# Linear attention on one core: all seven levels of a head prepared first, one run of score products, odd tiles of the coarsest level in the other column half

## The chip, the cores and the metric

The kernel runs on 1 core of one Trainium2 chip. The metric is device time in microseconds (us), the median of several runs. A core has a matrix engine (TensorE, in the profile PE, with its weight loads as PEld), a vector engine (VectorE, DVE), a scalar engine (ScalarE, ACT), a general engine (GpSimd, POOL) and a queue engine (SyncE, SP). They run side by side, each through its own queue in order, and wait for one another by semaphores. TensorE writes to PSUM, eight banks of 128 partitions by 512 float32 numbers; everything else lies in SBUF.

## The reference, cut to what matters

A decoder trunk of two layers on 512 tokens of width 1024, in float32. Each layer has a half-step SwiGLU feed-forward block, a mixer, and a second feed-forward block. The first layer's mixer is gated linear attention with 4 heads (128 key columns, 256 value columns), the second's is stick-breaking attention. The change is in the first mixer:

```python
bc = jnp.cumsum(to_chunks(log_a, GLA_HK), axis=3)      # per key column, a running log decay
...
o_inter = jnp.einsum('bhtk,bhkv->bhtv', q_t * jnp.exp(b_t), state)
diff = b_t[:, :, :, None, :] - b_t[:, :, None, :, :]
decay = jnp.exp(jnp.where(causal[:, :, None], diff, -jnp.inf))
scores = jnp.einsum('bhtk,bhtsk,bhsk->bhts', q_t, decay, k_t)
o_intra = jnp.einsum('bhts,bhsv->bhtv', scores, v_t)
```

The score of query t and key s is a sum over 128 key columns of q times k times exp(b_t - b_s), for s up to t. The decay differs by column, so the scores are not a plain product of two matrices unless the exponent is split at a reference point between s and t.

## The kernel before

**Tiles.** The kernel works on 4 tiles of 128 tokens (NT = 4), transposed: 128 key columns on the partitions, 512 tokens along the free axis. Within a tile of 128 the scores are a triangle of 128 by 128, and the kernel cuts it into *levels* (LEVELS = 64, 32, 16, 8, 4, 2, 1). At level B the tile falls into pieces of 2B tokens; the queries of a piece's second half meet the keys of its first half, and the last token of the first half is the reference. What is left is the diagonal, t = s.

**prepare(B)** (line 1164) makes one tile e of 128 by 512 for a level: two subtractions of b from its reference (lines 1172, 1173), an exponential on ScalarE (line 656, called from 1174), and two multiplications, the first halves by k and the second halves by q (lines 1175, 1176). Tiles named e come from a pool of 6 buffers with the tag "e", which the output's temporaries (kd, osq, sh, sl, vv) share.

**level(ps, e, B)** (line 1183) takes the score products. A bank of PSUM holds two levels, 256 columns each. For each of 4 tiles and each half of 64 keys (c = 0 or 64) one product of 128 by 64 weights with 64 columns is written to partitions c to c + 63, so that the two calls of a pair use the two column halves of the matrix engine. At level 64 only the first 64 tokens are keys, and there is one call a tile, with c = 0. Products are in float32, and a call shows as two rows in the profile, since the kernel's other products are of rounded high and low parts (float32r) that show as one.

**pick(ps, li)** (line 1189) copies, under a mask of zeros and ones, what a level gives into the score tile S (128 by 4 by 128) on VectorE. The diagonal is a product with the identity (line 1215), also on VectorE, and level 64 fills a block of 64 by 64 in each tile by a copy on ScalarE (line 1221).

**A head's turns.** levels(h) is a generator with 8 yields (n = 0 to 7), and the loop in run() (lines 1373 to 1399) puts work between them. At each n it runs one stretch of levels(h), then, from n = 1 on, one stretch of the previous head's output(), then one feed step: 24 products of the projections that are still to come (v, the gates). The feed keeps TensorE busy while VectorE prepares. Before the change the stretches are: n = 0 to 2 prepare levels 64, 32, 16; n = 3 takes the diagonal and these three levels in two z banks, prepares level 8, and empties the banks; n = 4 to 6 prepare levels 4, 2, 1; n = 7 takes the last four levels in two z banks and empties them.

**output(h)** (line 1235) runs one head later: kd and its exponentials, transposes of kd into the o bank (ps_kd, n = 3), the state products in the o bank and a z bank (ps_s, n = 5) with the running states on VectorE (lines 1279, 1281), the output products with S (ps_o, t banks, n = 7), then the norm (ps_on, o bank; vv, y, on). The last head's output has the output projection (ps_b) as its feed.

**PSUM.** Of the eight banks the tag a has 2, z 3, t 2 and o 1.

**Order.** The queues are laid out ahead of the run by a planner that simulates the engines: it goes by the order of the program, and where an instruction isn't ready by its own times it puts a later one first. Pieces of weights are cut into high and low parts by ScalarE (wh, line 152) and VectorE (wl, line 153) as the feed needs them.

Of the kernel before, what the change touches and what calls it, by code (L numbers as in the profile page):

```python
# [10 lines left out]
F32 = mybir.dt.float32  # L11
F32R = mybir.dt.float32r
# [6 lines left out]
P = 128  # L19
T = 512  # L20
# [3 lines left out]
NT = T // P  # L24
# [22 lines left out]
def decoder(ctx: ExitStack, tc: tile.TileContext, a: dict, out: bass.AP):  # L47
    nc = tc.nc
# [976 lines left out]
    class GLA:  # L1025
# [61 lines left out]
        def gate_weights(self):  # L1087

            gr = self.ep.tile([P, KD, 16], F32, tag="gr", bufs=1, name="gr")
            with nc.allow_non_contiguous_dma("gate columns"):  # L1090
                nc.gpsimd.dma_start(gr, cols(self.w_in, 3072, 16))
            self.gs = gs = self.ep.tile([P, KD, P], F32R, tag="gs", bufs=1, name="gs")
            nc.gpsimd.memset(gs.bitcast(F32), 0.0)
            nc.scalar.copy(gs[:, :, 0:16], gr)
            nc.vector.tensor_tensor(
                out=gs[:, :, 32:48], in0=gr, in1=gs[:, :, 0:16].bitcast(F32), op=ALU.subtract
            )

# [12 lines left out]
            one = self.ep.tile([P, 64], F32R, tag="one", bufs=1, name="one")[:, 0:1]  # L1111
            nc.scalar.copy(one, gT[:, 50:51])
            self.ones = one.to_broadcast([P, P])
            self.tri = self.ep.tile([P, P], F32, tag="tri", bufs=1, name="tri")
            nc.gpsimd.dma_start(self.tri, a["c_tri"])
            lf = self.ep.tile([P, len(LEVELS) * P // 2], F32, tag="e", name="lf")
            nc.gpsimd.dma_start(lf, a["c_lvl"])
            self.lvl = self.ep.tile([P, len(LEVELS) * P // 2], U8, tag="lvl", bufs=1, name="lvl")
            nc.vector.tensor_copy(self.lvl, lf)
            self.ga = self.gp.tile([P, T], F32R, tag="g", name="ga")  # L1120
            nc.gpsimd.memset(self.ga.bitcast(F32), 1.0)
# [7 lines left out]
        def gate_logits(self):  # L1129
            ga, t = self.ga, self.ep.tile([P, T], F32, tag="e", name="gl")  # L1130
            nc.vector.tensor_tensor(
# [25 lines left out]
        def levels(self, h):  # L1157
# [6 lines left out]
            def prepare(B):  # L1164
# [3 lines left out]

                e = self.ep.tile([P, T], F32, tag="e", name="e")
                (b0, b1), (e0, e1) = halves(b), halves(e)  # L1170
# [12 lines left out]
            def level(ps, e, B):  # L1183
                r = ps.rearrange("p (n m c) -> p n m c", n=NT, c=B)
                for i in range(NT):
                    for c in (0,) if B == H else (0, H):
                        mm(r[c : c + H, i], e[:, i * P + c : i * P + c + H], seconds(e, B)[:, i], True, True)

# [12 lines left out]
            es = []  # L1201
            for B in LEVELS[0:3]:
                es.append(prepare(B))
                yield
            halves = [t[:, c : c + T // 2] for t in (psum("ps_S", "z"), psum("ps_S", "z")) for c in (0, T // 2)]
            for i in range(NT):
# [3 lines left out]
            for ps, e, B in zip(halves[1:], es, LEVELS):  # L1210
                level(ps, e, B)
            es = [prepare(LEVELS[3])]
            for c in (0, H):
# [6 lines left out]
                )  # L1220
            nc.scalar.copy(S[0:H, :, H:P], halves[1][0:H].rearrange("p (n c) -> p n c", n=NT))
            pick(halves[2], 1)
            pick(halves[3], 2)
            yield
            for B in LEVELS[4:]:
                es.append(prepare(B))
                yield
            halves = [t[:, c : c + T // 2] for t in (psum("ps_S", "z"), psum("ps_S", "z")) for c in (0, T // 2)]
            for ps, e, B in zip(halves, es, LEVELS[3:]):
                level(ps, e, B)  # L1230
            for li, ps in enumerate(halves):
                pick(ps, li + 3)
            yield

        def output(self, h):
# [3 lines left out]
            bl = b.rearrange("p (n s) -> p n s", n=NT)[:, :, P - 1 : P]  # L1239
            kd = ep.tile([P, T], F32, tag="e", name="kd")  # L1240
            nc.vector.tensor_tensor(
# [46 lines left out]
            for vb in range(2):  # L1288
# [7 lines left out]
                po.append(ps)  # L1296
            sq, t = (ep.tile([P, T], F32, tag="e", name="osq") for _ in range(2))
# [4 lines left out]
            sh = ep.tile([P, T], F32R, tag="e", name="sh")  # L1302
            sl = ep.tile([P, T], F32R, tag="e", name="sl")
            nc.scalar.copy(sh, sq)
# [4 lines left out]
            mm(ps, self.ones, turns(sl), False, True)  # L1309
            vv = ep.tile([P, T], F32, tag="e", name="vv")  # L1310
            nc.vector.tensor_scalar(
# [687 lines left out]
```

## Time and profile before

| | us |
|---|---|
| median of 3 runs | 1762.55 |
| lowest and highest of these | 1762.22 and 1762.95 |
| the profiled execution | 1762.8 |
| its span, by the profile | 1760.9 |

All rows quoted below are from the profiled execution, and their times count from the start of its span. A row of a timeline has the start, the length, the engine, the line of the code, the operation, what is written from what, the shapes, and how many such instructions follow one another without a break; behind it stands, in brackets, how long the engine was idle just ahead and what ended that. Rows of products overlap, since a product starts before the one ahead has left the array; how fast they come is read from their starts. A row of stretches has the limits, the length, the busy time of each engine with its instructions, the granted clock of TensorE, and the DMA engines' share and rate. Rows of a group have the shortest, median and longest duration in ns.

### The profile page before, as it was taken

The numbers are of one execution on the slowest core, as the hardware profiler recorded it, in microseconds if no ns is written. First come the engines' busy times: TensorE is split into PE (matmuls) and PEld (weight loads), VectorE is DVE, ScalarE is ACT, GpSimd is POOL, SyncE is SP. The second block draws the span as 40 slices with busy tenths as digits, with TensorE's granted clock in tenths as the row PEclk, the third lists the DMA queues.
The fourth block names the chain that finished last, engine by engine and source line by source line (L and its number), as shares of the span: only waits on it lengthen the run. The fifth ranks groups of instructions, "written<-read, shape, count | busy, mean of one in ns | idle before, by whom it ended". The sixth has DMA issues, their size and how long they took to land.

```text
span 1760.9 us, 31387 instructions
## 1 busy us (share of the span) xinstructions
PE 1749.1 (99%) x12714; PEld 1631.3 (93%) x12714; DVE 1509.2 (86%) x2490; ACT 1063.8 (60%) x1899; POOL 55.6 (3%) x77
## 2 busy tenths in 40 slices
PE   9999999999999999999999999999999999999998
PEld 8999999889888999999989999999888889999997
DVE  8999797786888999889798988977898679998886
ACT  7556556554665565555655555655888755565555
POOL 0000000200000000000000000010000000000000
PEclk9999999999999999999999999999999999999999
DMA  5533435422123443444434344352212234434351
GB/s 169 155 113 116 134 107 148 116 65 70 60 79 113 122 118 121 120 121 126 128 98 134 103 126 129 106 133 84 84 49 73 72 96 132 126 102 124 117 146 52
DMA packets 186389, 193.14 MB, mean 110 GB/s; under 512 B 4931, under 2 KB 171125, under 8 KB 186245
## 3 DMA queue, kind: packets, MB, share of 16 engines
q1 hardware_dynamic: 177760, 175.91, 32.0%
q0 software_dynamic: 8240, 14.95, 4.7%
q8 instruction: 99, 1.62, 0.4%
q14 instruction: 46, 0.37, 0.1%
q10 hardware_dynamic: 244, 0.29, 0.0%
HBM read 175.17 MB, written 2.10 MB: 101 GB/s over the span
## 4 chain that ended last, share of the span: by engine, by line
PE 89%; DVE 7%; ACT 3%; DMA 1%; issue 1%; DVEq 0%; SPq 0%
PE ps_w L779 21%; PE ps_d L80 15%; PE ps_f L80 14%; PE ps_q L779 10%; PE ps_z L779 5%; PE ps_w L412 5%; PE ps_b L80 4%; PE ps_t L80 4%; PE ps_q L412 2%; PE ps_z L412 1%; DVE wl L153 1%; PE ps_z L1486 1%; PE ps_oT L1572 1%; PE ps_bt L80 1%; PE ps_T L1557 1%; DMA raw<-in_ffn_w_gate_dram 1%
## 5 line engine op out<-in xcount | busy, mean ns | idle before, releaser
L153 DVE TENSOR_TENSOR wl<-raw,wh 128x1024 fp32r<-128x1024 f32 x241 | 256.4, 1065 | 37.0 <-ACT wh L152 36.2
L152 ACT CAST wh<-raw 128x1024 fp32r<-128x1024 f32 x241 | 222.2, 923 | 70.0 <-PE ps_f L80 23.6
L153 DVE TENSOR_TENSOR wl<-s,wh 128x1024 fp32r<-128x1024 f32 x160 | 195.8, 1224 | 66.2 <-ACT wh L152 65.3
L779 PE MATMUL ps_w<-th,wh 128*128 128x256 f32 x864 | 239.1, 277 | 0.2 <-ACT ps_z L807 0.2
L779 PE MATMUL ps_w<-tl,wh 128*128 128x256 f32 x864 | 237.8, 275 | 0.0
L779 PE MATMUL ps_w<-th,wl 128*128 128x256 f32 x864 | 237.8, 275 | 0.0
L152 ACT CAST wh<-s 128x1024 fp32r<-128x1024 f32 x160 | 168.8, 1055 | 6.0 <-DVE s L765 6.0
L779 PEld LDWEIGHTS ps_w<-th,wh 128*128 128x128 f32 x864 | 165.9, 192 | 1.1 <-ACT ps_z L807 0.4
L80 PE MATMUL ps_f<-xh,wh 128*128 128x512 f32 x432 | 166.5, 386 | 0.0
L779 PEld LDWEIGHTS ps_w<-tl,wh 128*128 128x128 f32 x864 | 166.0, 192 | 0.0
L779 PEld LDWEIGHTS ps_w<-th,wl 128*128 128x128 f32 x864 | 166.0, 192 | 0.0
L80 PE MATMUL ps_f<-xh,wl 128*128 128x512 f32 x432 | 164.3, 380 | 0.5 <-DVE wl L153 0.5
L80 PE MATMUL ps_f<-xl,wh 128*128 128x512 f32 x432 | 164.0, 380 | 0.0
L80 PE MATMUL ps_d<-hh,wh 128*128 128x512 f32 x416 | 157.9, 380 | 0.0
L80 PE MATMUL ps_d<-hh,wl 128*128 128x512 f32 x416 | 157.8, 379 | 0.0
L80 PE MATMUL ps_d<-hl,wh 128*128 128x512 f32 x416 | 157.8, 379 | 0.0
L153 DVE TENSOR_TENSOR wl<-rawd,wh 128x1024 fp32r<-128x1024 f32 (+1 forms) x100 | 96.6, 966 | 9.7 <-ACT wh L152 9.7
L807 ACT COPY ps_z<-ps_w 128x256 f32<-128x256 f32 x72 | 26.0, 362 | 118.3 <-PE ps_w L779 118.1
L363 POOL DMA_DIRECT2D x<-d x53 | 46.0, 911 | 1552.1 <-ACT d L362 1093.5
L80 PEld LDWEIGHTS ps_f<-xl,wh 128*128 128x128 f32 x432 | 81.8, 189 | 11.4
L80 PEld LDWEIGHTS ps_f<-xh,wl 128*128 128x128 f32 x432 | 81.8, 189 | 11.3 <-DVE wl L153 0.9
L80 PEld LDWEIGHTS ps_f<-xh,wh 128*128 128x128 f32 x432 | 81.8, 189 | 10.7
(357 smaller groups left out, 5437.9 us busy)
## 6 DMA issues: line engine op xcount, KB each, us to landing
raw<-in_ffn_w_gate_dram SPq DMA_DIRECT2D x43, 1024.0 KB, 5.5
raw<-in_ffn_w_up_dram SPq DMA_DIRECT2D x43, 1024.0 KB, 5.4
rawd<-in_ffn_w_down_dram SPq DMA_DIRECT2D x84, 512.0 KB, 4.0
x<-d POOLq DMA_DIRECT2D x53, 256.0 KB, 4.6
raw<-in_gla_w_in_dram SPq DMA_DIRECT2D x12, 1024.0 KB, 5.3
raw<-in_sb_w_in_dram SPq DMA_DIRECT2D x16, 512.0 KB, 3.7
raw<-in_gla_w_out_dram SPq DMA_DIRECT2D x4, 1024.0 KB, 5.4
raw<-in_sb_w_in_dram SPq DMA_DIRECT2D x4, 1024.0 KB, 5.1
```

The lines of the kernel that those rows point to most:

```text
L80: st["pe"] = nc.tensor.matmul(ps, l, r, start=first, stop=last).ins
L152: nc.scalar.copy(h[:, k], part)
L153: nc.vector.tensor_tensor(out=l[:, k], in0=part, in1=h[:, k].bitcast(F32), op=ALU.subtract)
L363: nc.gpsimd.dma_start(xs[k], d, accum_op=ALU.add)
L412: st["pe"] = nc.tensor.matmul(ps, l_, r_, start=first and c + n == 0, stop=c == 1 and n == 2, skip_group_check=True).ins
L779: st["pe"] = nc.tensor.matmul(o, l_, r_, start=first and j + n == 0, stop=j == 3 and n == 2, skip_group_check=True).ins
L807: v["copied"] = nc.scalar.copy(z, w).ins
L1486: nc.tensor.matmul(o_, l_, r_, start=first, stop=last, skip_group_check=True)
L1557: nc.tensor.transpose(ps[:, c0 : c0 + P], ys[yb][:, yc + j * P : yc + (j + 1) * P], ident)
L1572: nc.tensor.matmul(po[e * 64 : e * 64 + 64, j * P : T], self.v[j][:, c : c + 64], self.wt[p, e][bk][:, c0 : c0 + n], start=j == 0, stop=j ...
```

## The change

All seven levels are prepared at n = 0 to 6, one at a time. At n = 7 the diagonal and all seven levels are multiplied in one run, into eight halves of four banks: three z banks and the o bank. Then the diagonal is written, ScalarE copies level 64, and the picks follow with levels 2 and 1 first (li = 5 and 6, the o bank), then levels 32 to 4.

Level 64 now writes the scores of tiles 1 and 3 to partitions 64 to 127, tiles 0 and 2 as before, so that its calls go to the two column halves in turn. The copy is in two pieces: even tiles from the lower partitions, odd tiles from the upper ones.

The pool with the tag "e" has 8 buffers in place of 6, which takes 4 KB more of each partition. Every use of the tag names the number.

```diff
-                e = self.ep.tile([P, T], F32, tag="e", name="e")
+                e = self.ep.tile([P, T], F32, tag="e", bufs=8, name="e")
...
             def level(ps, e, B):
                 r = ps.rearrange("p (n m c) -> p n m c", n=NT, c=B)
                 for i in range(NT):
-                    for c in (0,) if B == H else (0, H):
-                        mm(r[c : c + H, i], e[:, i * P + c : i * P + c + H], seconds(e, B)[:, i], True, True)
+                    for c in (0, H):
+                        if B < H:
+                            mm(r[c : c + H, i], e[:, i * P + c : i * P + c + H], seconds(e, B)[:, i], True, True)
+                        elif c == i % 2 * H:
+                            mm(r[c : c + H, i], e[:, i * P : i * P + H], seconds(e, B)[:, i], True, True)
...
             es = []
-            for B in LEVELS[0:3]:
+            for B in LEVELS:
                 es.append(prepare(B))
                 yield
-            halves = [t[:, c : c + T // 2] for t in (psum("ps_S", "z"), psum("ps_S", "z")) for c in (0, T // 2)]
+            halves = [t[:, c : c + T // 2] for t in (psum("ps_S", tag) for tag in "zzzo") for c in (0, T // 2)]
             for i in range(NT):
                 for c in (0, H):
                     s = slice(i * P + c, i * P + c + H)
                     mm(halves[0][c : c + H, i * H : i * H + H], k[:, s], q[:, s], True, True)
             for ps, e, B in zip(halves[1:], es, LEVELS):
                 level(ps, e, B)
-            es = [prepare(LEVELS[3])]
             for c in (0, H):
...
-            nc.scalar.copy(S[0:H, :, H:P], halves[1][0:H].rearrange("p (n c) -> p n c", n=NT))
-            pick(halves[2], 1)
-            pick(halves[3], 2)
-            yield
-            for B in LEVELS[4:]:
-                es.append(prepare(B))
-                yield
-            halves = [t[:, c : c + T // 2] for t in (psum("ps_S", "z"), psum("ps_S", "z")) for c in (0, T // 2)]
-            for ps, e, B in zip(halves, es, LEVELS[3:]):
-                level(ps, e, B)
-            for li, ps in enumerate(halves):
-                pick(ps, li + 3)
+            for c in (0, H):
+                to, of = (
+                    t.rearrange("p (n two) c -> p two n c", two=2)[:, c // H]
+                    for t in (S[0:H, :, H:P], halves[1][c : c + H].rearrange("p (n c) -> p n c", n=NT))
+                )
+                nc.scalar.copy(to, of)
+            for li in (5, 6, 1, 2, 3, 4):
+                pick(halves[li + 1], li)
             yield
```

The other lines of the diff give the same number of buffers to the other tiles of the tag (lf, gl, kd, osq, sh, sl, vv).

More of the change, by code (lines that the diff above doesn't have):

```diff
@@ L1115, in gate_weights @@
             nc.gpsimd.dma_start(self.tri, a["c_tri"])
-            lf = self.ep.tile([P, len(LEVELS) * P // 2], F32, tag="e", name="lf")
+            lf = self.ep.tile([P, len(LEVELS) * P // 2], F32, tag="e", bufs=8, name="lf")
             nc.gpsimd.dma_start(lf, a["c_lvl"])
@@ L1129, in gate_logits @@
         def gate_logits(self):
-            ga, t = self.ga, self.ep.tile([P, T], F32, tag="e", name="gl")
+            ga, t = self.ga, self.ep.tile([P, T], F32, tag="e", bufs=8, name="gl")
             nc.vector.tensor_tensor(
@@ L1239, in output @@
             bl = b.rearrange("p (n s) -> p n s", n=NT)[:, :, P - 1 : P]
-            kd = ep.tile([P, T], F32, tag="e", name="kd")
+            kd = ep.tile([P, T], F32, tag="e", bufs=8, name="kd")
             nc.vector.tensor_tensor(
@@ L1296, in output @@
                 po.append(ps)
-            sq, t = (ep.tile([P, T], F32, tag="e", name="osq") for _ in range(2))
+            sq, t = (ep.tile([P, T], F32, tag="e", bufs=8, name="osq") for _ in range(2))
             nc.scalar.activation(sq, po[0], AF.Square)
@@ L1301, in output @@
             yield
-            sh = ep.tile([P, T], F32R, tag="e", name="sh")
-            sl = ep.tile([P, T], F32R, tag="e", name="sl")
+            sh = ep.tile([P, T], F32R, tag="e", bufs=8, name="sh")
+            sl = ep.tile([P, T], F32R, tag="e", bufs=8, name="sl")
             nc.scalar.copy(sh, sq)
@@ L1309, in output @@
             mm(ps, self.ones, turns(sl), False, True)
-            vv = ep.tile([P, T], F32, tag="e", name="vv")
+            vv = ep.tile([P, T], F32, tag="e", bufs=8, name="vv")
             nc.vector.tensor_scalar(
```

## The prediction, made before the change was run

> **What bounds the kernel now.** I read the page first, then the busy time by stretches of the one stage that the change touches, then the order of time on TensorE and VectorE inside it.
>
> ```profile
> span 1760.9 us, 31387 instructions
> ...
> PE 1749.1 (99%) x12714; PEld 1631.3 (93%) x12714; DVE 1509.2 (86%) x2490; ACT 1063.8 (60%) x1899; POOL 55.6 (3%) x77
> ```
>
> TensorE is busy for 1749.1 of 1760.9 us, so a change is worth what it takes out of TensorE's own queue, or what it adds to it in waits. The linear-attention levels lie between 360 and 510 us. The next rows are stretches: length, then busy us of PE, weight load, DVE, ACT, POOL.
>
> ```profile
> 360.00:395.00 35.00, 35.00 (x302) 31.56 (x302) 34.17 (x74) 15.27 (x25) 0.00 (x0) 1.00 0.23 68
> 395.00:426.00 31.00, 31.00 (x354) 30.42 (x353) 15.75 (x28) 12.22 (x24) 0.31 (x1) 1.00 0.30 95
> 426.00:440.00 14.00, 13.73 (x161) 13.44 (x160) 13.86 (x31) 8.90 (x17) 0.00 (x0) 1.00 0.13 37
> 440.00:462.00 22.00, 22.00 (x193) 20.22 (x192) 15.65 (x29) 11.22 (x19) 0.00 (x0) 1.00 0.23 74
> 462.00:510.00 48.00, 47.37 (x331) 40.30 (x330) 47.81 (x91) 33.35 (x56) 0.00 (x0) 1.00 0.22 70
> ```
>
> TensorE is idle for 0.90 us of these 150 (0.27 in the third row, 0.63 in the fifth), and its granted clock is 1.00 throughout. VectorE is full in three of the five stretches: 34.17 of 35 (head 0), 13.86 of 14 (start of head 2) and 47.81 of 48 (head 3). TensorE is the bound, with VectorE close behind it in head 3. Idle time alone can give at most 0.9 us here; the rest must come out of how long TensorE takes for the score products.
>
> **The score products now.** Each call shows as two rows, so a head has 16 rows of the diagonal product, 8 of level 64 and 16 of each of six levels: 120. The change keeps all 120 (480 in four heads). The rows are start, length and count; the length holds the tail of the last product, so I subtract starts.
>
> ```profile
> 369.91 0.38 PE L80 MATMUL ps_f<-xh,wl 128*128 128x512 f32 x1
> 370.13 0.38 PE L80 MATMUL ps_f<-xl,wh 128*128 128x512 f32 x1
> 370.44 0.69 PE L80 MATMUL ps_S<-q,k 128*64 128x64 f32 x16
> 370.95 1.56 PE L80 MATMUL ps_S<-e 128*64 128x64 f32 x40
> 372.44 0.48 PE L80 MATMUL ps_f<-xh,wh 128*128 128x512 f32 x1
> 372.76 0.38 PE L80 MATMUL ps_f<-xh,wl 128*128 128x512 f32 x1
> ...
> 383.00 2.09 PE L80 MATMUL ps_S<-e 128*64 128x64 f32 x64
> 385.02 0.48 PE L80 MATMUL ps_f<-xh,wh 128*128 128x512 f32 x1
> ...
> 433.99 0.69 PE L80 MATMUL ps_S<-q,k 128*64 128x64 f32 x16
> 434.51 1.10 PE L80 MATMUL ps_S<-e 128*64 128x64 f32 x24
> 435.87 0.69 PE L80 MATMUL ps_S<-e 128*64 128x64 f32 x16 [0.27 <-DVE e L1176]
> 436.48 0.33 PE L1259 MATMUL ps_kd<-ident,kd 128*128 128x128 f32 x1
> ...
> 470.21 0.69 PE L80 MATMUL ps_S<-q,k 128*64 128x64 f32 x16
> 470.72 1.36 PE L80 MATMUL ps_S<-e 128*64 128x64 f32 x24
> 472.01 0.48 PE L80 MATMUL ps_f<-xh,wh 128*128 128x512 f32 x1
> ...
> 475.10 0.69 PE L80 MATMUL ps_S<-e 128*64 128x64 f32 x16
> 475.72 0.48 PE L80 MATMUL ps_f<-xl,wh 128*128 128x512 f32 x1
> ...
> 487.78 1.15 PE L80 MATMUL ps_S<-e 128*64 128x64 f32 x32
> 489.27 0.69 PE L80 MATMUL ps_S<-e 128*64 128x64 f32 x16 [0.33 <-DVE e L1176]
> 489.88 0.38 PE L80 MATMUL ps_o<-S,v 128*128 128x128 f32 x1
> ...
> 494.29 0.69 PE L80 MATMUL ps_S<-e 128*64 128x64 f32 x16
> 494.90 0.48 PE L80 MATMUL ps_f<-xl,wh 128*128 128x512 f32 x1
> ```
>
> Three prices come out of these.
>
> *A row.* 64 alternating rows take 385.02 - 383.00 = 2.02 us. A piece of 16 takes 494.90 - 494.29 = 0.61 us. A straight line through both gives 1.41 / 48 = 29.4 ns a row and 0.14 us for every piece, however long.
>
> *Level 64.* The first run of head 0 has 56 rows, 8 of them level 64, which all go to column half 0. It takes 372.44 - 370.44 = 2.00 us; the line gives 0.14 + 56 x 0.0294 = 1.79. The 8 rows thus cost 0.21 us more than 8 alternating ones, and I take it that alternating the halves saves that.
>
> *Coming and going.* Neighbouring ps_f rows start 370.13 - 369.91 = 0.22 us apart. Into the run it is 370.44 - 370.13 = 0.31, and after it 372.76 - 372.44 = 0.32: 0.09 and 0.10 us more, 0.19 for each piece that stands by itself among other products.
>
> **The change, part by part.**
>
> *One run of 120 rows* costs 0.14 + 120 x 0.0294 = 3.67 us.
>
> - Head 0 now: 2.00 + 2.02 = 4.02. Saved 0.35, and 0.19 for the piece that goes: 0.54.
> - Head 1: I take the same two runs, saved 0.35. Its first run stands directly ahead of the transposes (ps_kd), as head 2's does at 436.48. They stay where they are and now pay for coming and going alone, so no 0.19 here.
> - Head 2: its first run lasts 436.48 - 433.99 = 2.49 with the 0.27 us wait for a prepared tile. 2.49 + 2.02 - 3.67 = 0.84 saved, if the wait goes with the early run.
> - Head 3 is in four pieces: 1.80 + 0.62 + 2.10 + 0.61 = 5.13. VectorE is behind there, so I expect the last level to come apart again: 104 rows at 0.14 + 3.06 = 3.20, and 16 at 0.61. Saved 1.32, and 2 x 0.19 for the pieces at 470 and 475: 1.70.
>
> Together 0.54 + 0.35 + 0.84 + 1.70 = **3.4 us** off TensorE's queue.
>
> A page speaks against the level-64 term: the Trainium skill, "TensorE: Matmul & The Clock Gate", Part 3 (Packing small matmuls), states that a weight load overlaps running matmuls only when the row group differs. Two column halves of the same 128 rows would then gain nothing. The rows disagree: alternating ones come every 29.4 ns though one weight load alone lasts 132 to 139 ns, so I keep the term; what the rule would make of the time is a rival below.
>
> ```profile
> L80 PEld LDWEIGHTS ps_S<-e x416: 132/138/139, 370.9 to 494.7; 128*64 128x64 f32 x139
> L80 PE MATMUL ps_S<-e x416: 218/222/273, 371.0 to 494.8; 128*64 128x64 f32 x139
> L1191 DVE COPY_PREDICATED S<-lvl,ps_S x24: 427/476/766, 373.9 to 499.4; 128x256 f32<-128x256 uint8 x24
> L1215 DVE TENSOR_TENSOR S<-ps_S,ident x8: 408/424/428, 372.2 to 477.7; 64x256 f32<-64x256 f32 x8
> L1221 ACT COPY S<-ps_S x4: 349/365/366, 373.2 to 478.6; 64x256 f32<-64x256 f32 x4
> ```
>
> *VectorE* keeps its work: 24 picks, 8 diagonal products and 28 prepared tiles stay. They only move. Before the deadline of a head's last product it has 2 x 0.42 + 2 x 0.48 = 1.8 us less to do, and after it 6 picks and 2 diagonals in one lump: 6 x 0.48 + 0.84 = 3.7 us. Nobody on TensorE waits for S until the same head's output, one head later, so in heads 0 to 2 the lump costs nothing.
>
> *ScalarE* copies the level-64 block in two pieces of half the size. Between half of 0.365 each (nothing) and the whole of it each, that is 0 to 0.37 us a head. ScalarE is busy for 80.96 of the 150 us by the stretches above, so I take nothing; the upper end, 1.5 us for four heads, would count only if a weight cast behind it came late.
>
> *Eight buffers for e instead of six.* Seven tiles are now held until the run. A shortage of slots could delay the preparation, but the three tiles that used to wait for the first run's release no longer do. I take zero, between a gain of the 0.27 and 0.33 us waits (one of which the sum already holds) and the loss priced as the last rival. No DMA is added, and no queue of SP or POOL is passed.
>
> *Banks.* The run takes three z banks and the single o bank. The o bank is wanted next by the output norm (ps_on), which must now wait for the first two picks: 0.84 + 2 x 0.77 = 2.4 us after the run at their longest. In head 0 to 2 a feed step lies between, and a step is 24 rows of 0.22 us, so 5 us cover it. Without that cover, 2.4 us would be exposed.
>
> **What is late next.** In head 3 the cover is thin.
>
> ```profile
> 462.11 0.69 DVE L1074 TENSOR_TENSOR gn<-ps_f,R 128x512 f32<-128x512 f32 x1 [2.14 <-PE ps_f L80]
> ...
> 493.46 0.55 DVE L1176 TENSOR_TENSOR e<-e,q 128x256 f32<-128x256 f32 x1
> ...
> 501.60 2.35 DVE L153 TENSOR_TENSOR wl<-raw,wh 128x1024 fp32r<-128x1024 f32 x2
> ...
> 505.08 0.55 DVE L1248 TENSOR_TENSOR kd<-kd,k 128x384 f32<-128x384 f32 x1
> ...
> 505.78 0.41 PE L1259 MATMUL ps_kd<-ident,kd 128*128 128x128 f32 x2 [0.25 <-DVE kd L1248]
> ```
>
> VectorE starts this stretch when TensorE hands it a gate product (462.11, after 2.14 us of waiting) and is full until 505.6, where TensorE waits 0.25 us for kd. Heads 0 to 2 save 0.54 + 0.35 + 0.84 = 1.7 us, and they move VectorE's start with them. Head 3's own 1.7 us only counts if TensorE has something else to do when it gets to ps_kd early. It may: two weight pieces of the output projection are split by 503.95 (501.60 + 2.35), which is well over the 12 or so ps_b rows used up to then. I take a discount of 0.4 us for the places where it has not: 3.4 - 0.4 = **3.0 us**.
>
> The profiled execution took 1762.8 us (span 1760.9 and 1.9 around it), 0.25 over the median. Taken off the median, 1762.55 - 3.0 = **1759.5 us**.
>
> **Rivals.** About 0.2% (3.5 us) is what a measurement of this kernel can tell from no change; the signs below go by that, so faster starts at 1759.0 and slower at 1766.1.
>
> 1. *The full sum and the loose waits.* TensorE always has a filler, head 3's run holds together (0.14 + 0.19 more) and the waits of 0.33 and 0.25 us go. 3.4 + 0.9 = 4.3 at most, some 3.9 in the middle: **1758.6**. For it: the 2.14 us that VectorE waits at 462 and its half-empty stretches from 395 to 426 and from 440 to 462. Against: 47.81 of 48 in head 3.
> 2. *VectorE sets the end of head 3.* kd comes when VectorE is through, whatever TensorE saves there. Only the 1.7 us of heads 0 to 2 count, less 0.3 for the doubled lump ahead of kd: 1.4 saved, **1761.2**. For it: kd is the thing TensorE waits for at 505.78. The Trainium skill, "TensorEngine Tiling (Array Packing)", PSUM Bottleneck, warns of the same thing: tiling quickens TensorE but not the emptying of PSUM, which may then be the bound.
> 3. *The column half does nothing.* Then 8 rows a head keep their 0.21 us: 0.84 less than 3.0, so 2.2 saved, **1760.4**. By the rule on weight loads named above this is what would happen.
> 4. *Slower: TensorE stands at the joined run in head 3.* The queues are laid out ahead. If the run stays where the third piece is now (487.78, some 1.3 us earlier after the savings) but the seventh tile comes when it does now (493.46 + 0.55 = 494.0), TensorE waits 7.5 us in front of work it could have done. 7.5 - 3.4 = 4.1 lost: **1766.6**. It decides against the change from a wait of 3.4 us on. Against it: the layout now puts 24 rows of ps_o and some ps_f between the third piece and the last, so it knows of the delay, and VectorE has 1.8 us less to do before the seventh tile.
>
> **How the numbers follow.** Forecast 0.38 (own range 1759.0 to 1760.3), rival 1 0.33, rival 2 0.16, rival 3 0.04, rival 4 0.09. Faster by over 0.2% is rival 1: 0.33. Slower is rival 4: 0.09. The rest, forecast and rivals 2 and 3, is within 0.2%: 0.58. The range reaches from the end of rival 1 (4.6 saved, with 0.3 for the measurement and neighbours: 1757.9) over rival 2 to the case that nearly nothing comes through (0.2 saved: 1762.3); it leaves out rival 4 and the edges of the others.
>
> **What would show it.** *Right:* per head one run of 120 ps_S rows in about 3.7 us (head 3: 104 and 16), level-64 rows no denser than the rest, no wait of ps_S for e in head 2, kd near 503 us, ps_kd waiting under 0.5 us. *Wrong:* level-64 rows still 0.21 us longer (rival 3); ps_kd waiting 1 us or more for kd (rival 2); a ps_S row of head 3 with several us of idle time before it (rival 4); head 3's run in five or more pieces, each at 0.14 + 0.19 us; or VectorE's weight pieces (wl) behind the lump of picks, with TensorE's ps_f waiting for them.

## The result, and the profile after

The changed kernel takes 1760.03 us (median of 22 runs, 1759.46 to 1761.86), the kernel before 1762.53 us (22 runs). The ratio is 0.9987, with a 95% interval of 0.9981 to 0.9993: so 1.2 to 3.3 us were saved. The interval does not reach 1, so the saving is real, but it is under the 0.2% (3.5 us) at which the prediction let "faster" begin. I forecast 1759.5 us, "within 0.2%".

The head of the changed kernel's page, to be held against the two lines with which the prediction begins:

```profile
span 1758.0 us, 31376 instructions
...
PE 1746.1 (99%) x12714; PEld 1630.1 (93%) x12714; DVE 1509.0 (86%) x2490; ACT 1064.3 (61%) x1903; POOL 55.6 (3%) x77
```

No product went away (x12714 as before), yet TensorE is busy 3.0 us less in a span 2.9 us shorter. VectorE has the same work, and ScalarE four copies more. The gain has thus come out of TensorE's queue. Two of the five stretches of the prediction, the third and the fifth, with busy PE, PEld, DVE, ACT and POOL:

```profile
426.00:440.00 14.00, 14.00 (x128) 14.00 (x127) 14.00 (x34) 9.36 (x17) 0.00 (x0) 1.00 0.21 66
462.00:510.00 48.00, 47.29 (x340) 40.80 (x340) 47.92 (x92) 33.28 (x57) 0.00 (x0) 1.00 0.26 88
```

The idle 0.27 us of the third stretch is gone. The fifth, head 3, is as it was: both engines nearly full, and TensorE idle for 0.71 us (0.63 before).

TensorE's timeline of the changed kernel, in order of time. The first run is head 0's, the second head 2's; the rest is head 3.

```profile
380.88 0.69 PE L80 MATMUL ps_S<-q,k 128*64 128x64 f32 x16
381.40 3.21 PE L80 MATMUL ps_S<-e 128*64 128x64 f32 x104
384.54 0.48 PE L80 MATMUL ps_f<-xh,wh 128*128 128x512 f32 x1
...
447.83 0.69 PE L80 MATMUL ps_S<-q,k 128*64 128x64 f32 x16
448.34 3.21 PE L80 MATMUL ps_S<-e 128*64 128x64 f32 x104
451.48 0.71 PE L80 MATMUL ps_o<-S,v 128*128 128x128 f32 x4
...
459.89 0.38 PE L80 MATMUL ps_on<-sh,one 128*128 128x512 f32 x1
...
471.76 0.52 PE L1257 MATMUL ps_kd<-ident,kd 128*128 128x128 f32 x3 [0.47 <-DVE kd L1246]
...
484.31 0.69 PE L80 MATMUL ps_S<-q,k 128*64 128x64 f32 x16
484.83 1.34 PE L80 MATMUL ps_S<-e 128*64 128x64 f32 x40
486.10 0.49 PE L80 MATMUL ps_o<-eb,st 128*128 128x128 f32 x2
486.42 0.39 PE L80 MATMUL ps_o<-S,v 128*128 128x128 f32 x2
...
487.87 0.69 PE L80 MATMUL ps_S<-e 128*64 128x64 f32 x16 [0.18 <-DVE st L1279]
488.49 0.49 PE L80 MATMUL ps_o<-eb,st 128*128 128x128 f32 x2
...
489.80 1.15 PE L80 MATMUL ps_S<-e 128*64 128x64 f32 x32
490.88 0.49 PE L80 MATMUL ps_o<-eb,st 128*128 128x128 f32 x2
491.30 0.69 PE L80 MATMUL ps_S<-e 128*64 128x64 f32 x16
491.92 0.49 PE L80 MATMUL ps_o<-eb,st 128*128 128x128 f32 x2
...
520.60 0.38 PE L80 MATMUL ps_on<-sh,one 128*128 128x512 f32 x1
```

Heads 0 to 2 run as forecast: 120 rows from 380.88 to 384.54 are 3.66 us, and 451.48 - 447.83 is 3.65. Head 3 does not. Its run is in four pieces of 56, 16, 32 and 16 rows, with products of ps_o and ps_f between them, where I had two pieces of 104 and 16.

**Where the time went.** The norm products (ps_on) stand in every version and mark off the heads. A head's norm comes while the next head is in its levels: counted from the first gate product (ps_gk, at 344.45), head 0's ps_on comes after head 1's run, head 1's after head 2's, and the last one, head 3's own, at 520.60 (head 2's, at 496.78, is not used). I call these three starts marks. Head 3's stretch is the 60.71 us between the last two, from 459.89; it also holds the outputs of heads 2 and 3.

| us | before | after | saved | forecast |
|---|---|---|---|---|
| to the ps_on after heads 0 and 1 | 81.06 | 79.97 | 1.09 | 0.54 + 0.35 |
| from there over head 2 | 36.49 | 35.47 | 1.02 | 0.84 |
| from there over head 3 | 61.13 | 60.71 | 0.42 | 1.70, less 0.4 |
| all | 178.68 | 176.15 | 2.53 | 3.0 |

The 2.53 us of the stage are about the 2.50 of the medians; that they agree so closely is chance, since what comes behind the stage took 1237.43 us in one profiled execution of the changed kernel and 1237.97 in another. The table is a sum over TensorE's rows, and two profiled executions of the changed kernel put the last mark at 176.15 and 176.23, while its median moved by 0.5 us from one comparison to another. Below I therefore go by the stage first, and take differences of under 0.1 us there for nothing.

Head 3's stretch, each row counted to the start of the next, waits included:

| product | rows | before: us, pieces | after: us, pieces | saved |
|---|---|---|---|---|
| ps_S | 120 | 5.14, 4 | 4.10, 4 | 1.04 |
| ps_o | 56 | 5.86, 6 | 6.73, 10 | -0.87 |
| ps_f | 144 | 32.36, 9 | 32.14, 7 | 0.22 |
| ps_b | 60 | 14.05, 7 | 13.94, 7 | 0.11 |
| ps_kd | 6 | 0.55 | 0.63 | -0.08 |

The score products did save 1.04 us, and ps_o gave 0.87 back. A wait counts here for the row ahead of it. So 0.47 of the 0.87 is not ps_o's own: it is TensorE's wait at 471.76 for the kd of head 2, ahead of whose transposes the planner has put four rows of ps_o (from 470.68, 1.08 us with the wait). The other 0.40 is what ps_o costs in ten pieces in place of six, between the pieces of the run.

The kernel before, at the same transposes (its mark, VectorE's kd and TensorE's ps_kd), and then the changed kernel's kd:

```profile
461.91 0.38 PE L80 MATMUL ps_on<-sh,one 128*128 128x512 f32 x1
473.09 0.55 DVE L1248 TENSOR_TENSOR kd<-kd,k 128x384 f32<-128x384 f32 x1
473.79 0.52 PE L1259 MATMUL ps_kd<-ident,kd 128*128 128x128 f32 x3
```

```profile
471.07 0.54 DVE L1246 TENSOR_TENSOR kd<-kd,k 128x384 f32<-128x384 f32 x1
```

Kd is ready 473.64 - 461.91 = 11.73 us behind the mark in the kernel before and 471.61 - 459.89 = 11.72 in the changed one. The kernel before fills that time with head 3's early run (the 40 rows at 470.21, 1.80 us) and has no wait there. The joined run takes these rows away to 484, and TensorE comes to the transposes too soon.

### The profile page after: what moved, and what is told of

It reads as the page before. It is cut to its first block, busy times and chain, and to the rows that moved or that the text cites. A ratio compares the mean times of both kernels' runs of the same rounds, so it can differ in the third digit from the quotient of the medians.

```text
span 1758.0 us, 31376 instructions
## 1 busy us (share of the span) xinstructions
PE 1746.1 (99%) x12714; PEld 1630.1 (93%) x12714; DVE 1509.0 (86%) x2490; ACT 1064.3 (61%) x1903; POOL 55.6 (3%) x77
## 4 chain that ended last, share of the span: by engine, by line
PE 90%; DVE 6%; ACT 3%; issue 1%; DMA 1%; DVEq 0%; SPq 0%
PE ps_w L779 21%; PE ps_d L80 15%; PE ps_f L80 15%; PE ps_q L779 10%; PE ps_z L779 5%; PE ps_t L80 5%; PE ps_w L412 5%; PE ps_b L80 4%; PE ps_q L412 2%; DVE wl L153 1%; PE ps_z L1484 1%; PE ps_z L412 1%; PE ps_oT L1570 1%; PE ps_bt L80 1%; PE ps_T L1555 1%
```

## The experiments

Three theories for head 3. **Pieces:** the cut run and its fillers hold back what a whole run would save (rival: TensorE needs these fillers, and a whole run makes it wait). **VectorE:** VectorE sets the end of head 3, and nothing that TensorE saves there counts. **Banks:** a PSUM bank held by the state products cuts the run. For heads 0 to 2, that the column half saves nothing was still open, and so were the buffers. The edits are against the changed kernel, where nothing else is said. A stretch is head 3's, as in the table above.

| run | to ps_on after heads 0, 1 | after head 2 | after head 3 | stretch | time | ratio (95%) |
|---|---|---|---|---|---|---|
| before | 81.06 | 117.55 | 178.68 | 61.13 | 1762.53 | |
| after | 79.97 | 115.44 | 176.15 | 60.71 | 1760.03 | 0.9987 (0.9981 to 0.9993) |
| e1_one_half | 80.42 | 116.12 | 176.88 | 60.76 | 1760.89 | 0.9993 (0.9984 to 1.0001) |
| e2_halves_alone | 80.60 | 117.09 | 178.49 | 61.40 | 1762.10 | 0.9999 (0.9990 to 1.0008) |
| e3_buffers_alone | 81.06 | 117.55 | 178.68 | 61.13 | 1761.97 | 0.9997 (0.9989 to 1.0006) |
| e4_last_first | 79.96 | 115.45 | 176.79 | 61.34 | 1760.75 | 0.9991 (0.9982 to 1.0000) |
| e5_split_h3 | 79.96 | 115.44 | 177.37 | 61.93 | 1761.37 | 0.9996 (0.9987 to 1.0005) |
| e6_no_picks_h3 | 79.96 | 115.44 | 176.08 | 60.64 | 1759.98 | 0.9988 (0.9979 to 0.9997) |
| e7_seven | 79.96 | 115.44 | 176.24 | 60.80 | 1759.99 | 0.9988 (0.9979 to 0.9997) |
| e8_relief | 79.97 | 115.44 | 176.48 | 61.04 | 1760.17 | 0.9992 (0.9984 to 1.0001) |
| e9_state_in_t | 79.96 | 115.43 | 176.29 | 60.86 | 1760.42 | 0.9987 (0.9978 to 0.9997) |
| e10_out_behind | 79.96 | 115.43 | 176.97 | 61.54 | 1761.17 | 0.9993 (0.9985 to 1.0002) |
| after_again | 79.96 | 115.43 | 176.23 | 60.80 | 1760.53 | 0.9990 (0.9981 to 0.9999) |
| e12_six_levels_h3 | 79.97 | 115.44 | 175.49 | 60.05 | 1760.69 | 0.9992 (0.9983 to 1.0001) |

Each ratio is against the kernel before on the same chip, whose median lay between 1762.05 and 1762.53 us. The intervals of all versions with a joined run overlap, so the times alone put them in no order; the stretches, of one profiled execution each, do.

### One column half again

```diff
-                        elif c == i % 2 * H:
+                        elif c == 0:
...
-            for c in (0, H):
-                to, of = (
...
-                nc.scalar.copy(to, of)
+            nc.scalar.copy(S[0:H, :, H:P], halves[1][0:H].rearrange("p (n c) -> p n c", n=NT))
```

> The changed kernel with level 64 back in column half 0 for all four tiles (and one copy on ScalarE). My account: the 8 level-64 rows of a head cost 0.21 us more again, so each run of 120 takes about 3.89 us instead of 3.66, and the kernel is some 0.85 us slower than the changed one: about 1760.9. Rival 'the column half does nothing': runs of 3.66 us and 1760.0.

TensorE's timeline of this kernel in head 0:

```profile
380.69 0.69 PE L80 MATMUL ps_S<-q,k 128*64 128x64 f32 x16
381.20 3.44 PE L80 MATMUL ps_S<-e 128*64 128x64 f32 x104
384.57 0.48 PE L80 MATMUL ps_f<-xh,wh 128*128 128x512 f32 x1
```

The same 120 rows now take 384.57 - 380.69 = 3.88 us in place of 3.66. That is 0.22 a head for 8 rows, and 0.73 at the last mark: 0.45 in heads 0 and 1, 0.23 in head 2, and 0.05 in head 3. Alternating the halves does save in heads 0 to 2 what the prediction took for it. In head 3 next to nothing of it comes through. The Trainium skill, "TensorE: Matmul & The Clock Gate", Part 3, has weight loads overlap running matmuls only where the row group differs. These rows speak against that: all 128 rows of the array are used on both sides and only the column half changes, yet alternating rows come every 29.4 ns with a weight load of 138 ns each.

### The column half alone, on the kernel before

```diff
-                    for c in (0,) if B == H else (0, H):
-                        mm(r[c : c + H, i], e[:, i * P + c : i * P + c + H], seconds(e, B)[:, i], True, True)
+                    for c in (0, H):
+                        if B < H:
+                            mm(r[c : c + H, i], e[:, i * P + c : i * P + c + H], seconds(e, B)[:, i], True, True)
+                        elif c == i % 2 * H:
+                            mm(r[c : c + H, i], e[:, i * P : i * P + H], seconds(e, B)[:, i], True, True)
```

> The kernel before with the column halves of level 64 alternating, and nothing else. My account: the first run of head 0 takes 1.79 us instead of 2.00, four heads give 0.85 us: about 1761.7. Rival 'the column half does nothing': 1762.5. Rival 'the column half is the whole gain': 1760.0.

This expectation missed. Heads 0 and 1 give 0.46 us, head 2 gives nothing, and head 3 takes 0.27 back. At the last mark 0.19 us are left, and no difference in the time. Its timeline in head 2:

```profile
433.84 0.69 PE L80 MATMUL ps_S<-q,k 128*64 128x64 f32 x16
434.36 0.87 PE L80 MATMUL ps_S<-e 128*64 128x64 f32 x24
435.72 0.69 PE L80 MATMUL ps_S<-e 128*64 128x64 f32 x16 [0.49 <-DVE e L1176]
436.33 0.55 PE L1267 MATMUL ps_kd<-ident,kd 128*128 128x128 f32 x3
```

The first piece is quicker, and TensorE waits 0.49 us for the third tile where it waited 0.27. From 433.84 to 436.33 it is 2.49 us, exactly as before. What is saved ahead of a wait for VectorE is given back at that wait. In the changed kernel this wait is gone, and there e1 shows the halves worth 0.73. In head 3 the planner also lays the rows out in another order than in the kernel before, and TensorE waits 0.6 us for a state (ps_o), 0.3 for kd and 0.3 for a tile, where the kernel before has the 0.33 and 0.25 of the prediction.

### Eight buffers alone, and seven

The first takes `bufs=8` for the tag "e" into the kernel before, the second sets it to 7 in the changed one.

> The kernel before with 8 buffers for e instead of 6, and nothing else. My account: the gain is TensorE's own time in the score products, so buffers alone give 1762.5, within 0.5. Rival 'the buffers let VectorE prepare earlier and that is the gain': 1761.0 or less, and the wait of 0.27 us at head 2 is gone.

> The changed kernel with 7 buffers for e instead of 8, the fewest that the joined run can do with. My account: the buffers are only there so that seven tiles can stand at once; kd then takes one and the next tile waits for it. Heads 0 to 2 keep their runs of 3.66 us; 1760.0 to 1760.6. Rival 'the eighth buffer is where the gain is': 1761.5 or more.

Both came out as expected. All three marks of e3 are those of the kernel before, and e7's last mark, 176.24, is that of after_again, 176.23. The buffers make the order possible and cost or bring nothing.

### Head 3 in the old order

The changed kernel with the old split order in levels(3), column halves kept.

```diff
+            if h == 3:
...
+                for B in LEVELS[0:3]:
+                    es.append(prepare(B))
+                    yield
...
+                for B in LEVELS[4:]:
+                    es.append(prepare(B))
+                    yield
...
+                return
```

> The changed kernel with head 3 alone in the order of before (two runs of products, four picks each time), with its level 64 still in alternating halves. Theory 'VectorE sets the end of head 3': what the joined run takes off TensorE's queue there comes back as waits and fillers, so the kernel loses nothing by giving it up: 1760.0, within 0.4. Theory 'pieces' (the prediction's sum, 1.7 us of it in head 3): 1.0 to 1.5 slower, 1761.0 to 1761.5.

The stretch is 61.93 us, 1.22 longer than with the joined run, and the time lies in the range of "pieces". So VectorE does not simply set the end. But 1.22 is too much for what the joined run is worth, because the stretch is also 0.80 longer than in the kernel before, whose program has the same order there. The waits of TensorE between 460 and 521 us in this kernel (total, times, longest):

```profile
PE ps_o L80 <- DVE st L1321: 0.8, 2, 0.6
PE ps_kd L1299 <- DVE kd L1288: 0.3, 1, 0.3
PE ps_S L80 <- DVE e L1176: 0.3, 1, 0.3
```

All three are waits for VectorE, 1.4 us together. It is tempting to say that TensorE comes to VectorE too early, since heads 0 to 2 are 2.11 us quicker here. The traces do not show that. VectorE starts head 3 when TensorE hands it a gate product, 0.20 us behind the mark, in the kernel before (462.11 - 461.91), here and in the changed kernel alike.

The 0.80 have two parts. First, e2, which has the same order in head 3 and the alternating halves, but the old order in heads 0 to 2, has the same three waits (0.6, 0.3 and 0.3) and is 0.27 longer than the kernel before. Second, the other 0.53. From the mark on, e2 and e5 run the same operations in the same order on VectorE and ScalarE, and for the first 19 us each starts within 0.03 us of the same distance from the mark. They part at a piece of weights that ScalarE casts: its row in e5, and the load of that piece in e5 and in e2 (the last number is us from issue to landing).

```profile
480.19 1.05 ACT L152 CAST wh<-raw 128x1024 fp32r<-128x1024 f32 x1 [0.97 <-PE ps_s L1308]
raw<-in_gla_w_out_dram SPq DMA_DIRECT2D x1, 1024.0 KB, 6.3
```

```profile
raw<-in_gla_w_out_dram SPq DMA_DIRECT2D x1, 1024.0 KB, 5.1
```

The load is issued at 473.77 and lands 6.3 us later, at about 480.1, which fits the cast's start at 480.19. (The profile names ps_s, but in e2 the same cast starts while ps_s is still running.) In the kernel before, in e2 and in the changed kernel the same load takes 4.9 to 5.4 us, and this cast has no wait for it. Behind the late cast VectorE and TensorE are soon some 0.5 us later in e5 than in e2, and stay so to the end of the stretch.

So 0.53 of e5's stretch is a late load in its one profiled execution, and why it was late is not known. Without it the stretch would be that of e2, 61.40, and the joined run is worth some 61.40 - 60.71 = 0.7 us in head 3 (an estimate from these two stretches). Head 3's 0.42 is then 0.7 from the joined run, less the 0.27 that the alternating halves cost there in the old order. That coming to head 3 earlier costs anything is not shown.

### The run in one piece

e4 puts level 1, whose tile comes last, at the head of the run; e10 keeps the order and puts the output products behind it.

```diff
+            level(halves[7], es[6], LEVELS[6])
+            with tc.issue_after(st["pe"]):
...
-            for ps, e, B in zip(halves[1:], es, LEVELS):
+                for ps, e, B in zip(halves[1:7], es, LEVELS):
```

> The changed kernel with level 1, whose tile is prepared last, multiplied first, and the rest of the run laid out behind it, so that the run starts only when all seven tiles are there. Theory 'pieces': what head 3 kept back is the price of its run in four pieces, with the output products in small pieces between them (0.14 + 0.19 us a piece, 3 to 7 pieces): head 3's run is one piece of 3.66 us and the time falls by 1.0 to 1.5, to about 1758.8. Theory 'VectorE sets the end of head 3': the run is one piece, but the transposes of the last head (ps_kd) then wait that much longer for kd, and the time stays at 1760.0.

```diff
+            st["run"] = st["pe"]
...
+                    with behind(st["run"]):
+                        mm(ps[:, s], v[i][:, c0 : c0 + P], S[:, i], True, i == 0)
```

> The changed kernel with a head's output products (ps_o) laid out behind the next head's run, so that in head 3 they stand in one piece of 28 again as they do in heads 1 and 2 (3.15 us instead of 3.94 in six pieces). Theory 'pieces': 0.8 us off the stretch of 60.7 us, 1759.3. Theory 'order': the pieces were fillers for a time in which TensorE had to wait anyway; the stretch is the same or longer, as it was with the run in one piece (61.3): 1760.0 to 1760.7.

e4's timeline:

```profile
491.64 0.69 PE L80 MATMUL ps_S<-e 128*64 128x64 f32 x16
492.16 0.64 PE L80 MATMUL ps_S<-q,k 128*64 128x64 f32 x16
492.62 2.75 PE L80 MATMUL ps_S<-e 128*64 128x64 f32 x88
495.30 0.48 PE L80 MATMUL ps_f<-xh,wh 128*128 128x512 f32 x1
...
498.01 0.45 PE L80 MATMUL ps_on<-sh,one 128*128 128x512 f32 x1 [0.93 <-ACT wh L152]
```

The run is whole, 3.66 us, and the stretch is still 0.63 longer than after's. The products that stand between the pieces in the changed kernel have gone ahead of the run here, and behind it TensorE stands 0.93 us ahead of the norm. The profile puts this down to a weight's cast, the last thing to end. But ps_on does not read that weight. It needs sh, cast by 496.99, and the o bank, which the picks of levels 2 and 1 must empty first. Their row in e4, on VectorE:

```profile
496.37 1.49 DVE L1194 COPY_PREDICATED S<-lvl,ps_S 128x256 f32<-128x256 uint8 x2
```

They end at 497.86, and ps_on starts 0.15 us later, as ps_S does at 487.87 behind the state that frees its bank at 487.72. So the wait is most likely the one for the o bank that the prediction priced, "2.4 us after the run at their longest", with too little cover left behind the late run. The stretch from 460 to 521 us (PE's busy time is the second number after the limits), of after, e4 and e10 in turn:

```profile
460.00:521.00 61.00, 60.29 (x405) 52.37 (x404) 55.21 (x102) 40.59 (x68) 0.00 (x0) 1.00 0.21 70
```

```profile
460.00:521.00 61.00, 59.22 (x402) 51.18 (x401) 55.44 (x102) 40.60 (x67) 0.00 (x0) 1.00 0.22 70
```

```profile
460.00:521.00 61.00, 59.76 (x401) 51.27 (x401) 55.34 (x102) 40.54 (x67) 0.00 (x0) 1.00 0.21 70
```

TensorE is idle for 0.71, 1.78 and 1.24 us. In e10 ps_o is one block of 28 rows, the run is still in pieces, and the ps_kd of head 2 waits 0.92 us for kd where it waits 0.47 in the changed kernel, since no ps_o stands ahead of it; its stretch is 0.83 longer. Neither kernel came as "pieces" had it: e4 and e10 were expected at 1758.8 and 1759.3 us by that theory and took 1760.75 and 1761.17. The simple form of "pieces" falls: the pieces cost TensorE time in its queue, and taking them away costs more in waits. Nor did the last head's transposes wait for kd in e4, as "VectorE" had it.

### Work off VectorE

e6 takes the diagonal and the picks out of head 3; e8 moves a state copy and parts of the norm to ScalarE.

```diff
-            nc.gpsimd.memset(S[H:P, :, 0:H], 0.0)
+            nc.gpsimd.memset(S[H:P, :, 0:H] if h < 3 else S, 0.0)
...
-            for c in (0, H):
+            for c in (0, H) if h < 3 else ():
...
-            for li in (5, 6, 1, 2, 3, 4):
+            for li in (5, 6, 1, 2, 3, 4) if h < 3 else ():
```

> The changed kernel without the diagonal and the six picks of head 3 (its score tile is set to zero by GpSimd, so head 3's part of the attention within a tile is left out, but for level 64). VectorE has 2 x 0.42 + 6 x 0.5 = 3.8 us less to do ahead of kd. Theory 'VectorE sets the end of head 3': kd comes 3 to 4 us earlier, the output products of head 3 too, and the kernel is 0.7 us faster or more (as much as the waits and short pieces between 484 and 503 us hold): 1759.3 or less. Theory 'TensorE sets it': 1760.0, within 0.3, with kd earlier all the same.

```diff
-                    nc.vector.tensor_copy(s, o)
+                    (nc.scalar.copy if h == 2 else nc.vector.tensor_copy)(s, o)
...
+            if h in (1, 2):
+                nc.scalar.activation(pair(vv), flat(ps), AF.Copy, bias=EPS, scale=1.0 / 256)
...
+            if h in (1, 2):
+                nc.scalar.activation(vv, vv, AF.Copy, bias=1.5, scale=-0.5)
```

> The changed kernel with three operations of the outputs of heads 1 and 2 moved from VectorE to ScalarE: the norm's scale out of PSUM (0.60 us), the Newton step's 1.5 - 0.5 v (0.34) and the first state's copy (0.34, head 2 only), 2.2 us less for VectorE between 460 and 510 us. Theory 'VectorE sets the end of head 3': kd about 2 us earlier and 0.3 to 1.0 us faster, 1759.0 to 1759.7. Theory 'TensorE sets it': 1760.0, within 0.3.

The stretch from 460 to 521 us of e6, and VectorE's row of the last head's kd:

```profile
460.00:521.00 61.00, 60.23 (x405) 52.47 (x404) 52.34 (x94) 40.18 (x67) 0.00 (x0) 1.00 0.21 70
```

```profile
501.97 0.55 DVE L1246 TENSOR_TENSOR kd<-kd,k 128x384 f32<-128x384 f32 x1
```

VectorE does eight operations less and is busy 55.21 - 52.34 = 2.87 us less. It even stands idle for 0.80 us shortly ahead of kd. Yet kd starts only 0.47 us earlier (501.97 - 460.22 = 41.75 us behind e6's mark, 502.11 - 459.89 = 42.22 in the changed kernel), and the stretch is 0.07 us shorter. With e8, whose rows come 1.68 us later in its profile, VectorE is busy 48.23 us between 461.68 and 511.68, in place of 49.83 between 460 and 510, and the stretch is 0.33 longer. VectorE's amount of work does not set the end of head 3. There is a limit to this: e6 takes away only what comes behind the run, so it leaves the wait of 0.47 us for head 2's kd as it is, and in e8, where the planner makes that kd earlier, TensorE also comes to it earlier and waits 0.40. The Trainium skill, "TensorEngine Tiling (Array Packing)", PSUM Bottleneck, says that emptying PSUM may become the bottleneck once tiling quickens TensorE. It did not decide here: e6 empties seven halves of a bank less, in eight operations, and gains 0.07 us.

### The state products in another bank

```diff
-            ps, p2 = psum("ps_s", "o"), psum("ps_s", "z")
+            ps, p2 = psum("ps_s", "o"), psum("ps_s", "t" if h == 2 else "z")
```

> The changed kernel with the third state product of head 2's output (the one in a z bank, ps_s) in a t bank instead, so that all three z banks are free when head 3's run begins. Theory 'banks': the pair of levels that stood 29.9 us after the norm of head 1, for want of a bank that VectorE frees only at 29.5, goes with the first piece; head 3's run is in 3 pieces (88, 16, 16 rows) and the stretch from the norm of head 1 to that of head 3 (60.7 us in the changed kernel) is 0.4 to 0.8 us shorter: 1759.4. Theory 'tiles' (the last tile comes at 30.8 whatever the banks do, and other products fill the time): pieces as said, the stretch the same within 0.2: 1760.0.

VectorE's timeline of the changed kernel, first, shows what the pieces waited for:

```profile
486.91 0.46 DVE L1176 TENSOR_TENSOR e<-e,q 128x256 f32<-128x256 f32 x1
487.25 0.47 DVE L1279 SCALAR_TENSOR_TENSOR st<-st,el,ps_s 128x256 f32<-128x256 f32 x1
...
488.92 0.48 DVE L1279 SCALAR_TENSOR_TENSOR st<-st,el,ps_s 128x256 f32<-128x256 f32 x1
...
490.24 0.42 DVE L1176 TENSOR_TENSOR e<-e,q 128x256 f32<-128x256 f32 x1
...
502.11 0.55 DVE L1246 TENSOR_TENSOR kd<-kd,k 128x384 f32<-128x384 f32 x1
```

The diagonal and levels 64, 32 and 16 fill two z banks; they are the piece of 56 at 484.31. Level 2 goes to the o bank, which the second state frees at 487.25 + 0.47 = 487.72: the piece of 16 at 487.87, with its wait for st. Levels 8 and 4 go to the third z bank, which the third state frees at 489.40: the piece of 32 at 489.80. Level 1 needs the seventh tile, done at 490.66: the piece at 491.30. In e9 the third z bank is free early, levels 8 and 4 no longer stand alone, and 68 rows come together:

```profile
484.43 2.20 PE L80 MATMUL ps_S<-e 128*64 128x64 f32 x68
```

So the bank does decide where those 32 rows stand. But the run is not in the 3 pieces (88, 16 and 16 rows) that I expected. The planner has pulled 20 rows ahead, to both sides of head 2's transposes, where the changed kernel has ps_o; with the 68 and two of 16 it is in five pieces. The stretch is 60.86 us, no better than after_again's 60.80. "Banks" holds for the order and falls as a cost.

### Without the last level, and the changed kernel once more

e12 has no level 1 in head 3.

```diff
-                es.append(prepare(B))
+                if h < 3 or B > 1:
+                    es.append(prepare(B))
...
-            for li in (5, 6, 1, 2, 3, 4):
+            for li in (5, 6, 1, 2, 3, 4) if h < 3 else (5, 1, 2, 3, 4):
```

> The changed kernel without level 1 in head 3 (its tile isn't prepared, multiplied or picked; head 3's scores between neighbours are set to zero). TensorE has 16 rows less in a piece of their own, 0.62 us and 0.19 for coming and going: 0.8. VectorE has 4 x 0.34 us less ahead of the last product, whose tile then comes at 27.5 us after the norm of head 1 instead of 30.8. Theory 'the last tile sets head 3': the stretch from the norm of head 1 to that of head 3 falls from 60.7 us by 2 to 3.3, 1757 to 1758. Theory 'TensorE's own queue sets it' (the other products fill the time): it falls by 0.6 to 1.0, 1759.2.

> The changed kernel itself, beside the others on the same chip: 1760.0, and 60.7 us from the norm of head 1 to that of head 3.

The stretch is 60.05 us, 0.66 shorter: the 0.62 us that its 16 rows take (491.92 - 491.30 in the changed kernel), and little more. A last tile that set the end would have given up to 3.3: the seventh is done at 490.66, the sixth at 486.91 + 0.46 = 487.37. It also takes a prepared tile and a pick off VectorE, but e6 and e8 have shown that this alone brings nothing. The runs thus point to TensorE's own queue as the bound of head 3, in the pieces that it is cut into and with the wait for head 2's kd, which every version with a joined run in head 3 has (0.40 to 0.92 us). The whole time did not follow (1760.69 us). What comes behind the last mark takes 1237.43 us in the profiled execution of the changed kernel, 1237.97 in after_again and 1238.41 here; why it lost here stays open.

## Why the prediction was right, point by point

- **A row, a piece, the run.** 29.4 ns and 0.14 us gave 3.67 us for 120 rows; measured 3.66 and 3.65. The same line gives 1.79 for the 56 rows in head 3, and 486.10 - 484.31 is 1.79.
- **Level 64.** 0.21 us a head forecast, 0.22 by e1. Rival 3 (the half does nothing) falls.
- **Heads 0 to 2.** 1.73 forecast, 2.11 measured. Of head 1 I said that the transposes "now pay for coming and going alone, so no 0.19 here"; the same term is missing for head 2. Each head gave some 0.15 of it all the same: the transposes take 0.25 us alone (from 397.06) in place of 0.30 behind a run (from 399.64), and the ps_t rows around them 0.1 less.
- **Head 3: the step that failed.** "I expect the last level to come apart again: 104 rows [...] and 16", with 1.32 for the rows and 0.38 for two pieces, less 0.4. Measured: four pieces, as many as before. So the score products take 4.10 us in place of the 3.81 of the sum, and save 1.04. I named ps_on as the next to want the o bank; what cut the run was ps_s, which still held the o bank and one z bank. The 0.38 did come, as 0.40 in ps_f without its wait (7 pieces in place of 9). But the sum had no price for the products that fill the gaps: ps_o gave 0.40 back, and ps_b and ps_kd 0.14 and 0.08 without waits. In all 0.42 in place of 1.3.
- **The discount: right in size, by luck.** I took 0.4 for a wait at the last head's transposes. There is none there. The wait came at head 2's transposes (0.47), because the early run that used to stand ahead of them was gone, and at a bank (0.18); the 0.25 of before went, so that is 0.40 more.
- **Two errors that met.** Heads 0 to 2 were 0.38 too low and head 3 0.88 too high. Their sum, 0.5, is the miss of the forecast. That they have opposite signs is luck too, and the range, from 0.2 to 4.6 us saved, was too wide for the time to tell a right head 3 from a wrong one.
- **Zeros.** The buffers (e3, e7), the two copies on ScalarE and the lump of picks in heads 0 to 2 cost nothing that the runs show. In the whole stage, 340 to 560 us, TensorE of the changed kernel has three waits, and none is for a pick or for the bank of ps_on. (The first is for head 2's kd.)

```profile
PE ps_kd L1257 <- DVE kd L1246: 0.5, 1, 0.5
PE ps_b L80 <- DVE wl L153: 0.2, 1, 0.2
PE ps_S L80 <- DVE st L1279: 0.2, 1, 0.2
```

- **Signs.** The runs of 3.66 us in heads 0 to 2 and the end of the wait in head 2 came as named. The last head's kd was made at 502.11 + 0.55 = 502.66, near the 503 named, and its ps_kd follows without a recorded wait. The wait of 0.47 us is for head 2's kd, which no sign named. Head 3's run had four pieces, not the two of the forecast nor the five of the sign against it.
- **Rivals.** Rival 1 (full sum) needed a whole run without lost waits; e4 shows that a whole run brings waits. Rival 2 gave 1761.2 for nothing from head 3; 0.42 came; the last ps_kd has no wait, and e6 speaks against the mechanism. Rival 4 (TensorE stands) did not happen: the longest idle time ahead of a ps_S row is 0.18 us, since the planner put ps_o there.

No version that I ran beats the changed kernel. Open is whether another layout of head 3 can have both the short run and enough work ahead of head 2's transposes; none that I ran takes that wait away.

## What to carry to other kernels

A saving on the busiest engine counted in full while the next one had slack (heads 0 to 2), and shrank where both were full. Work that is joined into a later run leaves a hole where it stood: ask what used to wait behind it there, as head 2's transposes did. Before joining products into one run, list for each bank of the run who held it last, not only who wants it next. Products that fill a wait are worth their switching cost if the alternative is idle time; e4 and e10 had a cleaner queue and lost 0.6 and 0.8 us. Before a difference between two versions is called the price of a layout, lay their rows side by side from a common mark and find the first that differs: in e5 it was a late load.

## What was not expected of the hardware

- Products of 128 by 64 weights in alternate column halves come every 29 ns, though each row lasts 222 ns and its weight load 138. Eight rows on one half cost 0.22 us more, some 27 ns a row, so that each takes about twice the time.
- Small groups pay at each change of shape. Two ps_o rows take 0.32 us right behind a piece of ps_S (486.42 - 486.10) and 0.22 among their own kind (486.64 - 486.42). At 0.10 us each, the four more pieces of ps_o are the 0.40 us that they cost.
